# Value and output gate of a recurrent mixer's second half computed as one pair, with Strassen's scheme on two of eight chunks

## The chip, the cores and the metric

The kernel runs on one core of one Trainium2 chip. Its time is device time in microseconds (us) from the launch to the end of the program; "before" is the median of three runs. Besides there is one profiled execution, whose trace gives the start and the duration of each instruction of the engines: TensorE for matmuls (PE, its weight loads PEld), VectorE (DVE), ScalarE (ACT), GpSimd (POOL) and SyncE (SP), which here issues the transfers.

## What is computed

One layer of a decoder trunk on 256 tokens of 2048 features, all in float32. Cut to what matters:

```
h = rmsnorm(x, norm_mix_g)
u = h @ w_in                                  # 2048 x 12288
c_g, b_g, xa, za, q, fl, iv, og, ga, gb = split(u)
ya = b_g * causal_dwconv3(c_g * xa, conv_w) * silu(za)
o  = hgrn2_chunked(silu(q), kk, iv, log_f)    # kk and log_f from fl
yb = rmsnorm(o per head) * hg_norm_g * silu(og)
m  = sigmoid(ga) * (ya @ w_a_out) + sigmoid(gb) * (yb @ w_b_out)
x  = x + m @ w_o
x  = x + sigmoid(rmsnorm(x) @ w_ple_gate) * (p @ w_ple_proj)
return rmsnorm(x, final_norm_g)
```

The value `iv` and the output gate `og` of the recurrence are each 1024 wide. The kernel computes the eight fields of width 1024 in two halves of 512 columns.

## The kernel before, in words

**Groups, chunks, positions.** Each product with a weight matrix is cut into groups of 512 output columns, and a group into chunks of 256 rows of the weights (two k-tiles of 128). The list `groups` (lines 172 to 184) holds them in order: four projections PP, then f, q, iv, og, c, xa, za, b of the first half (j = 0), the same of the second half (j = 1), the merge gates ga and gb with the products A and B behind them, four groups O, and the late gates PG and GP. Each chunk is a position of `steps`; the main loop (line 1217) runs over the positions.

**Two halves of a number.** A float32 matrix is multiplied in three passes. `split` (lines 133 to 160) makes of a chunk of weights (128 x 1024) a rounded part `whi` on ACT (line 154) and the remainder `wlo` on DVE (line 155). The tokens exist as such a pair too. A plain chunk is 2 k-tiles x 2 token tiles x 3 matmuls (whi with xh, wlo with xh, whi with xl) of 128 x 128 by 512 columns, 12 in all (line 1156).

**Buffers and lead.** Raw weights come through three buffers of 1 MB (`load`, line 103), two chunks each. The pairs whi/wlo have four buffers in pool wp, so that a split waits until the matmuls of four positions before are over. `ahead` (line 1147) says how many positions the splits run ahead of the matmuls: LEAD = 3. In the range `gates` (line 212: from twelve positions before the first pair of merge gates to eight behind the last) a fifth pair of buffers is used, in the pool tmp2: at positions divisible by 5 (`more`, MORE = 1), and the lead is 4 there.

**Pairs by Strassen's scheme.** The merge gates ga and gb of j = 1, 2, 3 are computed together (kind GG, program GATES, line 42): two groups, eight chunks of rows. An entry such as `(0, 2)` is two plain chunks (2 and 3) of gate 0; an entry `("S", c)` is chunk c of both gates as a 2 x 2 block matrix (two k-tiles by two gates) times the 2 x 2 blocks of tokens, with seven products instead of eight, in four parts with 6, 3, 6 and 6 matmuls (`pair_products`, line 1166; its matmuls have line 1178). For it, `combine_weights` (line 162) makes differences and sums of the weight blocks on DVE (lines 166, 169, 170), in place and in a tile t2, and part 1 splits t2, half as wide. `forms_of_x` (line 750) loads the tokens of the chunks that are so treated, scales them on ACT (line 763) and makes four combinations and their pairs hi/lo on DVE and ACT (`forms`, lines 729 to 748). The products go to four accumulators "g" and four "s" in PSUM; `sums` (line 773) adds them up on DVE (line 769) as they become complete, after one copy on ACT (line 782), and hands each gate on.

**Epilogues.** When a group's last chunk is through, its epilogue starts as a generator; `advance` (line 1139) lets each one do a step per position (in an "S" entry at every second part), queued behind the newest split. `ep_iv` (line 405) scales the value into a tile v, `ep_og` (line 411) makes silu of the gate and goes over into `hgrn` (line 419), the recurrence of four heads: exponentials, element-wise products into tiles X (two of tag X, two of the ybT tiles, line 432), small matmuls on PE (lines 457, 590, 612 to 614), masks, norm, a turn through HBM, and the result ybT. It uses the tiles a, both, aoff (lines 437 to 441) and y (line 517) of pool tmp1. The second half's recurrence runs beside the groups c, xa, za, b.

The order of an engine's work is that of the program; the transfers are issued by SP in theirs (`ask_ahead`, line 1158).

Of the kernel before, what the change touches and what calls it, by code (L numbers as in the profile page):

```python
# [9 lines left out]
F32 = mybir.dt.float32  # L10
F32R = mybir.dt.float32r
# [4 lines left out]
P = 128  # L16
# [7 lines left out]
CW = 512  # L24
# [15 lines left out]


GATES = ("S", 0), (0, 2), ("S", 1), (1, 2), ("S", 4), (0, 6), ("S", 5), (1, 6)
LATE = (0, 4), ("S", 0), (0, 6), ("S", 1), (2, 3), ("S", 2), (1, 4), (1, 6)


# [6 lines left out]
def hybrid_kernel(ctx, tc, xT, x, pT, prm, gfin, masks, w_in, w_a, w_b, w_o, w_pg, w_pp, out):  # L52
# [28 lines left out]
    def nm(s):  # L81
        uid[0] += 1
        return f"{s}_{uid[0]}"
# [49 lines left out]
    def split(pos, c0=0, c1=2 * CW):  # L133
        part = part_of[pos]
        src = load(pos)[:, part % 2, :]
        if joint[pos]:

            src = load(pos)[:, part == 3, :]
            if part == 1:
                src, c1 = half[unit_of[pos]], CW  # L140

        pool, n = (pools["late"], 6) if (pos - state.get("late", len(steps))) % 10 < 6 and "late" in state else (wp, 4)
        if more(pos) and pos % (4 + MORE) < MORE:
            pool, n = pools[more(pos)], MORE
        if pos not in parts:
            parts[pos] = tuple(
                pool.tile([P, 2 * CW], F32R, tag=tag, bufs=n, name=nm(tag)) for tag in ("whi", "wlo")
            )
        hi, lo = parts[pos]
        s = slice(c0, c1)  # L150
        with ExitStack() as order:
            for i in state["before"].pop() if state.get("before") else ():
                order.enter_context(tc.issue_after(i))
            a = nc.scalar.activation(out=hi[:, s], in_=src[:, s], func=AF.Copy)  # L154
            v = nc.vector.tensor_tensor(  # L155
                out=lo[:, s], in0=src[:, s], in1=hi[:, s].bitcast(F32), op=ALU.subtract
            )
        state["splits"] = (a.ins, v.ins)
        if joint[pos] and part == 0:
            combine_weights(pos)  # L160

    def combine_weights(pos):

        b = load(pos).rearrange("p i (k c) -> p (i k) c", k=2)
        t2 = half[unit_of[pos]] = pools["tmp2" if pos in gates else "tmp3"].tile([P, CW], F32, tag="t2", bufs=2 if pos in gates else 1, name=nm("t2"))
        nc.vector.tensor_tensor(  # L166
            out=b[:, 0:4:3, :], in0=b[:, 0:3:2, :], in1=b[:, 3:4, :].to_broadcast([P, 2, CW]), op=ALU.subtract
        )
        nc.vector.tensor_tensor(out=t2, in0=b[:, 2, :], in1=b[:, 0, :], op=ALU.add)  # L169
        nc.vector.tensor_tensor(out=b[:, 1, :], in0=b[:, 1, :], in1=t2, op=ALU.subtract)  # L170
# [1 line left out]
    groups = []  # L172
    groups += [("PP", j, w_pp, j, "pT") for j in range(4)]
    for n, (kind, j) in enumerate(IN_ORDER):
        if j == 0 or kind not in ("ga", "gb"):
            groups.append((kind, j, w_in, n, "hT"))
        elif kind == "ga":
            groups.append(("GG", j, w_in, n, "hT", GATES))
        if kind == "gb":
            groups.append(("A", j, w_a, j, "yaT"))  # L180
            groups.append(("B", j, w_b, j, "ybT"))
# [24 lines left out]
    last_group = len(steps) - w_pg.shape[2]  # L206


    LEAD, MORE = 3, 1
    of_kind = lambda *kinds: [pos for pos, (gi, c) in enumerate(steps) if groups[gi][0] in kinds]  # L210
    gates, late = of_kind("GG"), of_kind("PG")[0]
    gates = range(gates[0] - 12, gates[-1] + 9)

    def more(pos):

        return "tmp2" if pos in gates else None

    TOKENS, NORM = 10, 13
    FIRST = 6

    praw = t4()[:, : 2 * T]
# [180 lines left out]
        plain_times(psum, sg, qt)  # L402
        state["qT", j] = yield from turned(qt, 5, t4("qT", 1))

    def ep_iv(j, psum):
        v = t4("v", 1)
        scaled(psum, v)
        state["v", j] = v
        yield
# [316 lines left out]
        yield  # L726


    def forms(op, pool, tag, r, chunks):


        n = len(chunks)
        f = t4()[:, : 4 * n * P]
        a11, a12, a21, a22 = (r[:, :, k, t * P : (t + 1) * P] for t in range(2) for k in range(2))
        s1, s2, s3, s4 = (f[:, i * n * P : (i + 1) * n * P].rearrange("p (u t) -> p u t", u=n) for i in range(4))
        nc.vector.scalar_tensor_tensor(out=s1, in0=a21, scalar=-1.0, in1=a22, op0=ALU.mult, op1=ALU.subtract)
        nc.vector.scalar_tensor_tensor(out=s2, in0=s1, scalar=-1.0, in1=a11, op0=ALU.mult, op1=ALU.subtract)
        yield
        nc.vector.tensor_tensor(out=s3, in0=a11, in1=a21, op=ALU.subtract)
        nc.vector.tensor_tensor(out=s4, in0=a12, in1=s2, op=ALU.subtract)  # L740
        yield
        hi, lo = (pool.tile([P, 4 * n * P], F32R, tag=tag + x, bufs=1, name=nm(tag + x)) for x in "hl")
        nc.scalar.activation(out=hi, in_=f, func=AF.Copy)
        nc.vector.tensor_tensor(out=lo, in0=f, in1=hi.bitcast(F32), op=ALU.subtract)
        for u in range(n):
            for i in range(4):
                s = slice((n * i + u) * P, (n * i + u + 1) * P)
                state["S", op, chunks[u], i] = hi[:, s], lo[:, s]

    def forms_of_x():  # L750

        joined = sorted(c for u, c in GATES if u == "S")
        for n in range(0, len(joined), 2):
            chunks = joined[n : n + 2]
            raw = t4()
            r = raw.rearrange("p (u k t) -> p u k t", u=2, k=2)
            for u in range(2):
                nc.sync.dma_start(out=r[:, u], in_=xT[:, 2 * chunks[u] : 2 * chunks[u] + 2, :])
            for u in range(2):
                yield  # L760
                for k in range(2):
                    h = r[:, u, k, :]
                    nc.scalar.activation(out=h, in_=h, func=AF.Identity, scale=gain(PRM_GMIX, 2 * chunks[u] + k))
            yield
            yield from forms("hT", pools["tmp2"], f"Sx{n}", r, chunks)
            yield

    def add(out, x, y):
# [32 lines left out]
    def ep_pair(j, e, left):  # L801

        def tiles_of():
            state["ga", j], state["gb", j] = t4("ga", 1), t4("gb", 1)
            return state["ga", j], state["gb", j]

        def then(q, g):
            for t in range(NT):
                s = slice(t * CW, (t + 1) * CW)
                nc.scalar.activation(  # L810
                    out=g[:, s], in_=g[:, s], func=AF.Sigmoid, scale=state["rstd1"][:, t : t + 1]
                )

        yield from sums(e, left, tiles_of, then)

    def ep_a(j, psum):
        g = state["ga", j]
# [26 lines left out]
    def ep_o(j, psum):  # L844
# [18 lines left out]
        if j < 2:  # L863
            for c in range(4):
                h = x1[:, c * T : (c + 1) * T]
                nc.scalar.activation(out=h, in_=h, func=AF.Identity, scale=gain(PRM_GPLE, j * 4 + c))
            hi, lo = (x[:, j * 4 : j * 4 + 4, :].rearrange("p k t -> p (k t)") for x in state["x1T"])
            nc.scalar.activation(out=hi, in_=x1, func=AF.Copy)
            nc.vector.tensor_tensor(out=lo, in0=x1, in1=hi.bitcast(F32), op=ALU.subtract)
            yield  # L870
            chunks = [c for u, c in LATE if u == "S" and c // 2 == j]
            r = x1.rearrange("p (u k t) -> p u k t", u=2, k=2)[:, : len(chunks)]
            yield from forms("x1T", pools["tmp3"], f"So{j}", r, chunks)
            return
        for c in range(4):
            put(state["x1T"], j * 4 + c, x1[:, c * T : (c + 1) * T], gain(PRM_GPLE, j * 4 + c))
# [269 lines left out]

    def ahead(pos):

        return LEAD + min(max(pos - late - 4, 0) // 3, 5) + MORE * (more(pos + LEAD) is not None and more(pos + LEAD + MORE) == more(pos + LEAD))

    def product(psum, op, k, t, hi, lo, first, last, which=(0, 1, 2)):

# [64 lines left out]
    for pos, (gi, c) in enumerate(steps[:last_group]):  # L1217
# [25 lines left out]
            load_x(pos + 2)  # L1243
        if pos == 4:
            begin()
        if 0 <= pos - NORM < 4:
            add_squares(pos - NORM)
        if pos == NORM + 3:
# [5 lines left out]
        if program:  # L1254
            program = program[0]
            if c == (0, 0):
                total = products_of(program)
                left, banks = dict(total), {}
            if c == (min(n for n, (u, _) in enumerate(program) if u == "S"), 0):
                active.append({"GG": ep_pair, "GP": ep_gates_late}[kind](j, banks, left))  # L1260
            pair_products(c, program, opname)
            ask_ahead()
            if not joint[pos] or c[1] % 2:
                advance()
            if kind == "GP" and c in ((1, 1), (3, 1)):
                load_projection(1 + c[0] // 2)
            continue
# [32 lines left out]
        if c == nch - 1:  # L1300
# [3 lines left out]
            if kind == "ga" and j == 0:  # L1304
                finish()
                second_part()
                active.append(forms_of_x())
                step(active[-1])
            if kind == "O" and j == 0:
                state["x1T"] = operand(big, "x", KT)  # L1310
# [103 lines left out]
```

## Time and profile before

| | |
|---|---|
| runs before (median, lowest, highest) | 814.6, 814.54, 814.64 us |
| the profiled execution, its own time | 814.02 us |
| its span, first to last instruction | 812.2 us |
| granted TensorE clock, mean | 0.996 |
| PE, PEld, DVE, ACT, POOL busy | 802.9, 667.5, 625.9, 463.5, 91.1 us |
| HBM read, written | 173.97 MB, 13.63 MB |

Spans are counted from the first instruction. A row of the timeline gives the start, the time taken, engine, line and operation, then what is written and what is read, with shapes; in brackets stands how long the engine was idle before and what released it. A row with x3 or the like is several instructions merged. In the views by group the last numbers are busy time, mean duration and idle time ahead of the group. Matmuls overlap in the trace, so that a duration of 0.39 us is no measure of their pace; the distance of their starts is.

### The profile page before, as it was taken

Reading aid. Unit: us, or ns where it says so; the run is one execution under the profiler, and the core shown is the slowest. Engines: PE = TensorE matmul, PEld = TensorE weight load, DVE = VectorE, ACT = ScalarE, POOL = GpSimd, SP = SyncE. Lnnn points to the kernel's source line nnn. Section 1 sums busy time; section 2 is a strip of 40 time slices with the busy share of each in tenths; the row PEclk is TensorE's granted clock in tenths of the full one; section 3 lists DMA queues with packets and bytes.
Section 4 is the critical chain, followed back from the end, with each engine's and each line's share of the span. In section 5 each row is a group of like instructions: output and inputs, shape, how many; then the busy total and the mean of one; then the engine's idle time right before and its main releaser. Section 6 shows DMA issues by size and latency. Waiting matters only on the chain.

```text
span 812.2 us, 10984 instructions
## 1 busy us (share of the span) xinstructions
PE 802.9 (99%) x4199; PEld 667.5 (82%) x4199; DVE 625.9 (77%) x737; ACT 463.5 (57%) x607; POOL 91.1 (11%) x74
## 2 busy tenths in 40 slices
PE   9999999999999999999999999999999999999995
PEld 7888888888888888888888888888888888888885
DVE  5747697967766488967767998998997657679895
ACT  7667465555555465565664554564564456665652
POOL 1000045400000055200001000100100000002012
PEclk9999999999999999999999999999999999999998
DMA  9979656747767555647764774774866687887542
GB/s 339 372 276 342 224 170 208 230 167 238 257 234 255 184 185 201 214 155 261 271 239 146 225 268 148 250 258 157 259 230 230 215 304 245 295 301 270 201 144 105
DMA packets 46565, 188.33 MB, mean 232 GB/s; under 512 B 5296, under 2 KB 14768, under 8 KB 31408
## 3 DMA queue, kind: packets, MB, share of 16 engines
q1 hardware_dynamic: 46368, 187.36, 67.5%
q8 instruction: 33, 0.54, 0.3%
q10 hardware_dynamic: 144, 0.26, 0.1%
q14 instruction: 20, 0.16, 0.1%
HBM read 173.97 MB, written 13.63 MB: 231 GB/s over the span
## 4 chain that ended last, share of the span: by engine, by line
PE 88%; DVE 5%; DMA 3%; ACT 1%; issue 1%; SPq 0%; POOL 0%; ACTq 0%; POOLq 0%; DVEq 0%
PE g L1156 70%; PE g L1178 11%; PE s L1178 4%; DMA raw<-in_w_pg 2%; DVE wlo L155 2%; PE s L1156 1%; PE s L457 1%; ACT whi L154 1%; DVE raw L166 1%; DMA raw<-in_w_pp 0%; DVE t L920 0%; DVE xs L921 0%; DMA turn<-t 0%; DVE t L169 0%; DVE t L938 0%
## 5 line engine op out<-in xcount | busy, mean ns | idle before, releaser
L155 DVE TENSOR_TENSOR wlo<-raw,whi 128x1024 fp32r<-128x1024 f32 (+1 forms) x310 | 384.4, 1255 | 156.3 <-ACT whi L154 154.9
L154 ACT ACTIVATE whi<-raw 128x1024 fp32r<-128x1024 f32 (+1 forms) x310 | 320.0, 1049 | 250.7 <-PE g L1156 197.4
L1156 PE MATMUL g<-wlo,xh 128*128 128x512 f32 (+1 forms) x656 | 251.9, 384 | 0.0
L1156 PE MATMUL g<-whi,xl 128*128 128x512 f32 (+1 forms) x656 | 251.7, 384 | 0.0
L1156 PE MATMUL g<-whi,xh 128*128 128x512 f32 (+1 forms) x656 | 251.6, 385 | 0.0
L1156 PEld LDWEIGHTS g<-whi,xh 128*128 128x128 f32 x656 | 123.3, 188 | 24.5
L1156 PEld LDWEIGHTS g<-whi,xl 128*128 128x128 f32 x656 | 123.3, 188 | 24.5
L1156 PEld LDWEIGHTS g<-wlo,xh 128*128 128x128 f32 x656 | 123.3, 188 | 24.0
L1178 PE MATMUL g<-wlo,xh 128*128 128x512 f32 x166 | 64.6, 389 | 0.0
L1178 PE MATMUL g<-whi,xl 128*128 128x512 f32 x166 | 64.6, 389 | 0.0
L1178 PE MATMUL g<-whi,xh 128*128 128x512 f32 x166 | 64.4, 389 | 0.0
L1156 PE MATMUL g<-whi,mh 128*128 128x512 f32 x128 | 49.8, 389 | 0.0
L1156 PE MATMUL g<-wlo,mh 128*128 128x512 f32 x128 | 49.8, 389 | 0.0
L1156 PE MATMUL g<-whi,ml 128*128 128x512 f32 x128 | 49.6, 389 | 0.0
L154 ACT ACTIVATE whi<-t 128x512 fp32r<-128x512 f32 x15 | 9.5, 632 | 54.4 <-DVE t L169 54.4
L1178 PEld LDWEIGHTS g<-whi,xl 128*128 128x128 f32 x166 | 31.2, 188 | 6.5
L1178 PEld LDWEIGHTS g<-whi,xh 128*128 128x128 f32 x166 | 31.2, 188 | 6.5
L1178 PEld LDWEIGHTS g<-wlo,xh 128*128 128x128 f32 x166 | 31.1, 188 | 6.4
L832 POOL TENSOR_TENSOR t<-ga,gb 128x512 f32<-128x512 f32 x6 | 10.6, 1786 | 192.9 <-issue 118.1
L1156 PEld LDWEIGHTS g<-whi,ml 128*128 128x128 f32 x128 | 24.0, 188 | 5.0
L1156 PEld LDWEIGHTS g<-wlo,mh 128*128 128x128 f32 x128 | 24.0, 188 | 5.0
L1156 PE MATMUL g<-whi,yaTh 128*128 128x512 f32 (+1 forms) x74 | 28.0, 385 | 0.1
(250 smaller groups left out, 919.8 us busy)
## 6 DMA issues: line engine op xcount, KB each, us to landing
raw<-in_w_in SPq DMA_DIRECT2D x73, 1024.0 KB, 5.0
raw<-in_w_in SPq DMA_DIRECT2D x34, 512.0 KB, 6.6
raw<-in_w_o SPq DMA_DIRECT2D x16, 1024.0 KB, 6.0
raw<-in_w_pg SPq DMA_DIRECT2D x12, 1024.0 KB, 6.4
turn<-t SPq DMA_DIRECT2D x72, 128.0 KB, 2.7
t<-turn SPq DMA_DIRECT2D x18, 512.0 KB, 5.4
raw<-in_w_a SPq DMA_DIRECT2D x8, 1024.0 KB, 5.2
raw<-in_w_b SPq DMA_DIRECT2D x8, 1024.0 KB, 5.3
```

Of the source, the lines that this page charges most:

```text
L154: a = nc.scalar.activation(out=hi[:, s], in_=src[:, s], func=AF.Copy)
L155: v = nc.vector.tensor_tensor(out=lo[:, s], in0=src[:, s], in1=hi[:, s].bitcast(F32), op=ALU.subtract)
L166: nc.vector.tensor_tensor(out=b[:, 0:4:3, :], in0=b[:, 0:3:2, :], in1=b[:, 3:4, :].to_broadcast([P, 2, CW]), op=ALU.subtract)
L457: nc.tensor.matmul(heads(bk)[r, h, c if at is None else slice(at, at + 32)], key(h)[:, r], query(h)[:, c], start=True, stop=True, tile_pos ...
L832: (nc.vector if j == 3 else nc.gpsimd).tensor_tensor(out=spread(m, t), in0=blocks(ga[:, s]), in1=blocks(gb[:, s]), op=ALU.add)
L1156: nc.tensor.matmul(psum, a, b, start=first and n == 0, stop=last and n == 2)
L1178: nc.tensor.matmul(banks[name], x, y[:, s], start=k == total[name] and i == 0, stop=k == 1 and i == 2)
```

## The change

The groups iv and og of the second half (j = 1) become one pair of kind VG with the program INNER: chunks 0 and 1 by Strassen's scheme, the other six of each plain, 20 positions in place of 16. `forms_of_x` takes the program and its target as arguments; for VG it runs from the sixth position before the pair and writes into the half of yaT that is still unused. The tiles t2 lie in the recurrence's tiles both and aoff. A new epilogue `ep_inner` lets `sums` add up, and hands the value to `ep_iv` (scaled in place) and the gate to `ep_og`, both now from SBUF.

In a range `inner`, from six positions before the pair to its end, three more pairs whi/wlo are used at three of seven positions: the two X tiles, a with y, and the two ybT tiles of the second half. `ahead` lets the lead grow there from 3 to 6 by steps (position + LEAD must have reached the range's start, two and four positions behind it). `MORE` becomes a table: one pair for `gates`, as before, three for `inner`. Positions behind the pair move by four.

Its core:

```diff
+INNER = (0, 2), (0, 4), ("S", 0), (0, 6), ("S", 1), (1, 2), (1, 4), (1, 6)
...
-        if more(pos) and pos % (4 + MORE) < MORE:
-            pool, n = pools[more(pos)], MORE
+        places = [(pool, n, tag) for tag in ("whi", "wlo")]
+        n = len(MORE[more(pos)])
+        if pos % (4 + n) < n:
+            places = [(pools[name], 1 + (tag == "X"), tag) for name, tag in MORE[more(pos)][pos % (4 + n)]]
...
+        if more(pos) == "inner":
+            pool, tag, n = "tmp1", ("both", "aoff")[unit_of[pos] // 2 % 2], 1
...
-        if j == 0 or kind not in ("ga", "gb"):
+        if (kind, j) == ("iv", 1):
+            groups.append(("VG", j, w_in, n, "hT", INNER))
+        elif (kind, j) == ("og", 1):
+            continue
+        elif j == 0 or kind not in ("ga", "gb"):
...
-    LEAD, MORE = 3, 1
+    LEAD = 3
+    MORE = {
+        None: (), "gates": ((("tmp2", "whi"), ("tmp2", "wlo")),),
+        "inner": (
+            (("tmp1", "X"), ("tmp1", "X")), (("tmp1", "a"), ("tmp1", "y")), (("branch", "ybTh1"), ("branch", "ybTl1")),
+        ),
+    }
...
+    inner = of_kind("VG")
+    inner = range(inner[0] - 6, inner[-1] + 1)
...
-        return "tmp2" if pos in gates else None
-
-    TOKENS, NORM = 10, 13
+        return "gates" if pos in gates else "inner" if pos in inner else None
+
+    TOKENS, NORM, FORMS = 10, 13, inner[0]
...
-    def ep_iv(j, psum):
-        v = t4("v", 1)
+    def ep_iv(j, psum, v=None):
+        v = t4("v", 1) if v is None else v
...
+    def ep_inner(j, e, left):
+
+        def then(q, g):
+            halves = [g[:, A], g[:, B]]
+            after = ep_og(j, halves) if q else ep_iv(j, halves, g)
+            next(after)
+            active.append(after)
+
+        yield from sums(e, left, lambda: (t4("v", 1), t4()), then)
...
-        return LEAD + min(max(pos - late - 4, 0) // 3, 5) + MORE * (more(pos + LEAD) is not None and more(pos + LEAD + MORE) == more(pos + LEAD))
+        at, n = more(pos + LEAD), 0
+        while n < len(MORE[at]) and more(pos + LEAD + n + 1) == at and (at == "gates" or pos + LEAD >= inner[0] + 2 * n):
+            n += 1
+        return LEAD + min(max(pos - late - 4, 0) // 3, 5) + n
...
+        if pos == FORMS:
+            held = [x[:, 4:, :].rearrange("p k t -> p (k t)") for x in state["yaT"]]
+            active.append(forms_of_x(INNER, lambda n: lambda: held))
+            step(active[-1])
...
-                active.append({"GG": ep_pair, "GP": ep_gates_late}[kind](j, banks, left))
+                active.append({"GG": ep_pair, "GP": ep_gates_late, "VG": ep_inner}[kind](j, banks, left))
```

More of the change, by code (lines that the diff above doesn't have):

```diff
@@ L142, in split @@
         pool, n = (pools["late"], 6) if (pos - state.get("late", len(steps))) % 10 < 6 and "late" in state else (wp, 4)
-        if more(pos) and pos % (4 + MORE) < MORE:
-            pool, n = pools[more(pos)], MORE
+        places = [(pool, n, tag) for tag in ("whi", "wlo")]
+        n = len(MORE[more(pos)])
+        if pos % (4 + n) < n:
+            places = [(pools[name], 1 + (tag == "X"), tag) for name, tag in MORE[more(pos)][pos % (4 + n)]]
         if pos not in parts:
             parts[pos] = tuple(
-                pool.tile([P, 2 * CW], F32R, tag=tag, bufs=n, name=nm(tag)) for tag in ("whi", "wlo")
+                pool.tile([P, 2 * CW], F32R, tag=tag, bufs=n, name=nm("w" + x)) for (pool, n, tag), x in zip(places, ("hi", "lo"))
             )
@@ L164, in combine_weights @@
         b = load(pos).rearrange("p i (k c) -> p (i k) c", k=2)
-        t2 = half[unit_of[pos]] = pools["tmp2" if pos in gates else "tmp3"].tile([P, CW], F32, tag="t2", bufs=2 if pos in gates else 1, name=nm("t2"))
+        pool, tag, n = ("tmp2", "t2", 2) if pos in gates else ("tmp3", "t2", 1)
+        if more(pos) == "inner":
+            pool, tag, n = "tmp1", ("both", "aoff")[unit_of[pos] // 2 % 2], 1
+        t2 = half[unit_of[pos]] = pools[pool].tile([P, CW], F32, tag=tag, bufs=n, name=nm("t2"))
         nc.vector.tensor_tensor(
@@ L726, in ep_gb, with forms @@
         yield
-    def forms(op, pool, tag, r, chunks):
+    def forms(op, made, r, chunks):
         n = len(chunks)
@@ L741, in forms @@
         yield
-        hi, lo = (pool.tile([P, 4 * n * P], F32R, tag=tag + x, bufs=1, name=nm(tag + x)) for x in "hl")
+        hi, lo = made()
         nc.scalar.activation(out=hi, in_=f, func=AF.Copy)
@@ L748, in forms, with form_tiles, forms_of_x @@
                 state["S", op, chunks[u], i] = hi[:, s], lo[:, s]
-    def forms_of_x():
-        joined = sorted(c for u, c in GATES if u == "S")
+    def form_tiles(pool, tag, n=2):
+        return lambda: tuple(pool.tile([P, 4 * n * P], F32R, tag=tag + x, bufs=1, name=nm(tag + x)) for x in "hl")
+    def forms_of_x(program, made):
+        joined = sorted(c for u, c in program if u == "S")
         for n in range(0, len(joined), 2):
@@ L764, in forms_of_x @@
             yield
-            yield from forms("hT", pools["tmp2"], f"Sx{n}", r, chunks)
+            yield from forms("hT", made(n), r, chunks)
             yield
@@ L872, in ep_o @@
             r = x1.rearrange("p (u k t) -> p u k t", u=2, k=2)[:, : len(chunks)]
-            yield from forms("x1T", pools["tmp3"], f"So{j}", r, chunks)
+            yield from forms("x1T", form_tiles(pools["tmp3"], f"So{j}", len(chunks)), r, chunks)
             return
@@ L1306, in hybrid_kernel @@
                 second_part()
-                active.append(forms_of_x())
+                active.append(forms_of_x(GATES, lambda n: form_tiles(pools["tmp2"], f"Sx{n}")))
                 step(active[-1])
```

## The prediction

> **What bounds the kernel now.** The page comes first. Under the span stand each engine's busy time, its share of the span and its instructions.
>
> ```profile
> span 812.2 us, 10984 instructions
> ...
> PE 802.9 (99%) x4199; PEld 667.5 (82%) x4199; DVE 625.9 (77%) x737; ACT 463.5 (57%) x607; POOL 91.1 (11%) x74
> ```
>
> A busy PE proves little by itself, so the second view is that of the waits of PE (engine, line, what it waited for, us in total, times, longest), the third the chain that ended last (start, us, what).
>
> ```profile
> PE s L1034 <- PEq L1403: 0.8, 1, 0.8
> ```
>
> ```profile
> 178.21 138.73 PE g L1156 x612
> ...
> 359.11 84.33 PE g L1156 x372
> 443.44 0.68 PE s L1178 x3
> ...
> 478.80 5.44 PE g L1178 x24
> 484.24 21.76 PE g L1156 x96
> ...
> 609.36 108.59 PE g L1156 x479
> ```
>
> PE waits once in the whole execution, 0.8 us for its warm-up at the start. From 178 to 718 the chain is PE behind PE: no transfer and no split of weights is late. (The rest of the chain passes over other engines, but the waits view has no further wait of PE.) So the pace of the matmuls sets the end, and the pace is in the chain: 21.76 / 96 = 0.2267 us for one of 512 columns, and 84.33 / 372 gives the same. Nothing but fewer matmuls can shorten this kernel there, and any wait of PE is added in full.
>
> The Trainium skill, "Perfetto Trace Analysis", section Identifying the Most-Contended Engine, says that the busy share of matmuls is no good measure and that weight-load busy time is a better one; by it the 82% of PEld leaves headroom, and fewer matmuls might return nothing. The trace agrees that 99% proves little, but the waits view and the constant 0.2267 us speak against headroom here.
>
> **The gain.** A plain chunk of 256 rows for two gates takes 2 k-tiles x 2 token tiles x 2 gates x 3 (hi/lo) = 24 matmuls; by Strassen's scheme it is seven products, 21. The trace already holds the same thing: the pair of gates from 443.44 to 484.24 has four such chunks of eight and takes 40.80 us, where two plain groups take 2 x 21.76 = 43.52: 2.72 us for four, 0.68 each. Two chunks: 6 x 0.2267 = **1.36 us**.
>
> The Trainium skill, "TensorE: Matmul & The Clock Gate", section Back-to-back issue gap, gives some 131 ns for a sustained matmul of 512 columns; by it six would be an estimated 0.79 us and the time 813.8. The row of this kernel decides: 0.2267.
>
> **What it costs.** All of it is on DVE, ACT and SP, so it costs nothing unless a split comes late. The windows (us, then busy time and count of PE, PEld, DVE, ACT and POOL, granted TensorE clock, DMA share, GB/s) are: today's value and output gate; the recurrence of the second half with the four groups beside it; the existing pair.
>
> ```profile
> 240.63:284.15 43.52, 43.52 (x194) 36.04 (x192) 25.61 (x23) 22.87 (x26) 1.96 (x1) 1.00 0.66 218
> 284.15:378.00 93.85, 93.85 (x697) 78.16 (x696) 76.07 (x95) 55.44 (x84) 29.03 (x20) 1.00 0.59 196
> 443.28:484.08 40.80, 40.80 (x181) 33.78 (x180) 38.53 (x39) 24.36 (x27) 3.53 (x2) 1.00 0.73 244
> ```
>
> The added instructions have rows in the existing pairs: subtraction, T2 and third combination (L166, L169, L170), the half-size split, the sums (L769), the copy out of PSUM (L782), the forms of x (L736 to L744, L763) and their load (L758). First the groups of the existing pair's window (count, busy us, mean ns, idle before and its releaser), then one line's own view (ns min/median/max), rows of the timeline (start, us), and the groups of the window of value and output gate.
>
> ```profile
> L166 DVE TENSOR_TENSOR raw<-raw 128x1024 f32<-128x1024 f32 x3 | 3.7, 1225 | 0.1
> ...
> L155 DVE TENSOR_TENSOR wlo<-t,whi 128x512 fp32r<-128x512 f32 x3 | 2.1, 692 | 0.2
> L169 DVE TENSOR_TENSOR t<-raw 128x512 f32<-128x512 f32 x3 | 2.1, 692 | 0.1
> L170 DVE TENSOR_TENSOR raw<-raw,t 128x512 f32<-128x512 f32 x3 | 2.1, 692 | 0.1
> L154 ACT ACTIVATE whi<-t 128x512 fp32r<-128x512 f32 x3 | 1.9, 632 | 12.5 <-DVE t L169 12.5
> ```
>
> ```profile
> L769 DVE TENSOR_TENSOR gb<-gb,s x9: 681/683/1218, 479.5 to 609.8; 128x512 f32<-128x512 f32 x6, 128x1024 f32<-128x1024 f32 x3
> ```
>
> ```profile
> 406.73 1.70 ACT L763 ACTIVATE t<-t,prm_t 128x256 f32<-128x256 f32 x4
> ```
>
> ```profile
> 408.46 0.43 DVE L736 SCALAR_TENSOR_TENSOR t<-t 128x256 f32<-128x256 f32 x1 [0.18 <-ACT t L763]
> ...
> 413.08 1.22 DVE L744 TENSOR_TENSOR Sx0l<-t,Sx0h 128x1024 fp32r<-128x1024 f32 x1
> ```
>
> ```profile
> L155 DVE TENSOR_TENSOR wlo<-raw,whi 128x1024 fp32r<-128x1024 f32 x17 | 20.8, 1224 | 17.7 <-ACT whi L154 17.5
> L154 ACT ACTIVATE whi<-raw 128x1024 fp32r<-128x1024 f32 x16 | 16.9, 1059 | 19.6 <-PE g L1156 19.6
> ```
>
> DVE: combining 2 x (1.225 + 2 x 0.692) = 5.2; each chunk's splits are three and a half instead of four, 2 x (0.692 - 1.224) = -1.1; sums 6 x 0.683 + 1.22 = 5.3; forms 4 x 0.43 + 1.22 = 2.9, of which the load's place (sixth position before the pair) puts nearly all ahead of the window. Together 12.3: 25.6 + 12.3 = 37.9 us if all fell into the new window of 42.16, 90%. The existing pair runs at 38.53 of 40.80, 94%, with one extra pair of tiles, and PE doesn't wait there. ACT gains 1.70 + 1.06 (L743, by the whi of its shape) + 0.63 (L782, by a half-size whi) - 2 x (1.059 - 0.632) = 2.5 on 22.9. Price: nothing while this cover holds; with it gone, each us that a split is late is a us of PE.
>
> How much cover, before the added lead? The last fence, of the window of value and output gate, says it: ACT idled 19.6 us, all of it until PE gave a buffer back, and DVE 17.7 us behind ACT. The splits are as early as four pairs of tiles allow. Three more pairs raise the lead from three positions to six (it grows at positions 75, 77 and 79, while the pair begins at 84), 3 x 12 x 0.2267 = 8.2 us more. DVE's burst in a Strassen chunk is 3 x 1.224 + 0.692 + 2.6 = 7.0 us for 21 x 0.2267 = 4.8 us of PE; two chunks fall behind by 4.4 us, with a plain unit (5.4 us of PE, 2.4 of DVE) between them to catch up.
>
> The added wait: ACT's half-size whi waits for T2 (12.5 us over three in the row above, some 4 each); behind it in ACT's queue stand the next two splits and the epilogues, and DVE waits for those. Two of them are 8 us of ACT's free 19.6, spread over a lead of as much. Taken as nothing; bounds 0 and 8, the range keeps a part.
>
> **SP and the forms' load.** Bytes of weights are the same; each Strassen chunk is three issues instead of one, and two transfers of x are new.
>
> ```profile
> 397.31 0.90 SPq L758 DMA_DIRECT2D t<-in_xT  x2
> ```
>
> ```profile
> DMA to landing us min/median/max: 5.3/5.6/5.8
> ```
>
> Two issues take 0.9 us on SP and land after 5.3 to 5.8. The gain of x stands on ACT one position (2.72 us) behind the issue, so ACT may wait about 3 us, with the splits of the pair's first chunks behind it. PE then holds splits of five positions, 13.6 us. Nothing, then; the forms are needed some eleven positions later.
>
> **What the tiles cost elsewhere.** The first half's recurrence ends with the puts of ybT, the second's begins with y:
>
> ```profile
> 208.02 1.67 DVE L266 SCALAR_TENSOR_TENSOR ybTl<-t,prm_t,ybTh 128x256 fp32r<-128x256 f32 x4
> ```
>
> ```profile
> 287.39 1.22 DVE L518 TENSOR_TENSOR y<-b,tot 128x1024 f32<-128x1024 f32 x1
> ```
>
> Between these X, a, y, both and aoff are dead, as are the second half of yaT and the second ybT pair. The new pair's last use of them is over before 284; its first (positions 78 and 79, split some three to four positions ahead) comes after 208. The recurrence begins one position later against its neighbours, since the last two sums (2 x 0.68) stand ahead of its gate. What is late next there?
>
> ```profile
> 332.00 1.21 DVE L155 TENSOR_TENSOR wlo<-raw,whi 128x1024 fp32r<-128x1024 f32 x1
> ```
>
> ```profile
> 337.35 0.39 PE L1156 MATMUL g<-whi,xh 128*128 128x512 f32 x1
> ```
>
> ```profile
> 313.23 0.41 DVE L493 TENSOR_TENSOR X<-t,qT 128x256 f32<-128x256 f32 x1
> ```
>
> ```profile
> 316.95 1.29 PE s L457 x96
> ```
>
> The tightest split of that stage ended at 333.2 and PE took it at 337.35: 4.1 us. The tightest input of its own small matmuls, X, was ready 3.3 us early. Its matmuls move with it, so that distance stays. 1.4 us more DVE work fits into both. Value: 0, bounds 0 and +1.
>
> The sum, against the profiled execution: 814.02 (span 812.2) - 1.36 = 812.66. That execution lay 0.58 under the median of 814.6 (runs 814.54 to 814.64), so for a median: 814.6 - 1.36 = **813.24**, 0.17% less.
>
> **The rivals.**
>
> *A burst too dense* (PE waits in the new pair, under 3 us in all). For it: 7.0 us of DVE for 4.8 of PE. Against: 4.4 us of arrears against 8.2 us of added lead and a stage that is 59% busy now. It would eat the gain, at the likeliest 1 to 1.4 us: 814.2 to 814.6.
>
> *No headroom used:* PE's pace isn't what ends last there, and six matmuls return nothing: 814.6. The 2.72 us of the existing pair speak against it.
>
> *The three later pairs lose their lead* (slower). They have almost no reserve:
>
> ```profile
> 453.52 4.63 DVE L155 TENSOR_TENSOR wlo<-raw,whi 128x1024 fp32r<-128x1024 f32 x4 [0.46 <-ACT whi L154]
> ```
>
> ```profile
> 455.52 0.39 PE L1178 MATMUL s<-whi,Sx0h 128*128 128x512 f32 x1
> ```
>
> The first of these four splits ends near 454.75 and PE uses it at 455.52: 0.77 us. The program grows by four positions, and which position gets the fifth pair of tiles is counted by position modulo 5, so their turn falls one position later against the chunks. If that cost them one plain position of lead, each would wait 2.72 - 0.77 = 1.95 us: 814.6 - 1.36 + 3 x 1.95 = **819.1**. It decides from 0.77 us on. Against: five pairs in rotation give the same lead in whatever phase once they all turn, and the stage is entered twelve positions after they begin.
>
> **How the numbers follow.** Forecast (no new wait) 0.82, own range 812.9 to 813.7; dense burst 0.08; no headroom 0.03; lost lead 0.07. For 8 in 10 the forecast's own range nearly does; with half of the burst it is 812.9 to 814.2. What a measurement can tell from no change is taken as 0.2%, 1.63 us, so the border of faster is 812.97, only 0.27 below the forecast, about half of what the profiled execution lay from the median. Faster gets 0.10 out of the forecast's 0.82; the other 0.72, the burst and no headroom make same 0.83; lost lead is slower, 0.07.
>
> **What would show it.** Right: PE's instructions 4199 - 6 = 4193, the new pair's 186 matmuls in 42.16 us, still one wait of PE in the waits view, DVE 12 us busier in all. Wrong: a wait of PE for wlo L155 or an X in 238 to 285, a chain that leaves PE before 700, or a wait in the three later pairs; or matmuls whose distance isn't 0.2267.

## The result, and the profile after

The changed kernel is slower: 817.88 us (817.45 to 818.38, six runs) against 814.57 (814.38 to 814.68, six runs) of the kernel before beside it, ratio 1.0041 with an interval of 1.0028 to 1.0054. The forecast was 813.24 with a range of 812.9 to 814.2: the wrong side, and out of the range by 3.7 us. (The profiled executions lie 4.36 us apart, 818.38 and 814.02. Of this 0.93 us is there before any changed work has run: the first small matmul of the recurrence starts at 136.90 us, before at 135.97. That is the spread of the start; e4 below, the same up to there, has 136.06.)

The page of the changed kernel, span and engines:

```profile
span 816.6 us, 11017 instructions
...
PE 805.5 (99%) x4193; PEld 666.2 (82%) x4193; DVE 637.2 (78%) x759; ACT 468.3 (57%) x617; POOL 91.9 (11%) x74
```

PE has six matmuls fewer, 4193, and DVE is 11.3 us busier in all: the work is what was counted. Yet PE is busy for 2.6 us more, with less to do, while the weight loads fell by 1.3: a part of each late start counts as busy, as is worked out below. PE's waits (engine, line, what it waited for, us in total, times, longest):

```profile
PE g L1214 <- DVE wlo L158: 1.0, 2, 0.7
PE s L1067 <- PEq L1443: 0.8, 1, 0.8
PE g L1192 <- issue: 0.4, 1, 0.4
PE s L1214 <- DVE wlo L158: 0.2, 1, 0.2
PE g L1192 <- ACT mh L871: 0.2, 1, 0.2
PE g L1214 <- ACT whi L157: 0.2, 1, 0.2
```

One row has become six, of which one, that of the warm-up, was there before. (Lines have moved: the split is 157 and 158, a pair's matmuls 1214, plain ones 1192.) Where the waits are, the chain that ended last tells. It is PE behind PE up to the new pair, leaves PE inside it and comes back to PE there (start, us, what):

```profile
241.72 8.17 PE g L1214 x36
...
250.88 1.56 ACT whi L157 x2
...
263.97 0.70 DVE t L175
264.77 0.63 ACT whi L157
...
271.27 16.16 PE g L1214 x70
```

From 250 to 271 the chain runs over ACT and DVE, the splits, and back to PE. The window of the pair (us, then busy time and count of PE, PEld, DVE, ACT, POOL, granted clock, DMA share, GB/s), from its first matmul to the first behind it:

```profile
241.56:287.27 45.71, 44.18 (x188) 34.30 (x186) 36.38 (x42) 23.07 (x28) 5.28 (x4) 1.00 0.54 185
```

45.71 us for 186 matmuls, not 42.16: **3.55 us lost here**, at full clock. The waits view shows only 1.4 us of that for line 1214. A matmul's record is 0.39 us long while the next may start after 0.2267, so up to 0.16 us of each late start is covered by the record of the matmul before. The Trainium skill, "Perfetto Trace Analysis", section Summary: the profiler window per engine type, says that the end of a TensorE record is an estimate; the trace agrees, and the distance of starts is the measure.

Two smaller losses lie elsewhere. Four late starts between 650.91 and 653.11, in the first output group, make 0.83 us, and one in the group za 0.57, each beyond the pace. Six matmuls fewer, and 3.55 + 0.83 + 0.57 more, would be 3.59 us; the medians differ by 3.31.

**The main loss.** ACT in the changed kernel around the pair's first Strassen chunk:

```profile
240.95 1.06 ACT L762 ACTIVATE yaTh<-t 128x1024 fp32r<-128x1024 f32 x1 [0.78 <-DVE t L759]
247.19 1.06 ACT L157 ACTIVATE whi<-raw 128x1024 fp32r<-128x1024 f32 x1 [5.18 <-PE g L1214]
249.91 2.01 ACT L157 ACTIVATE whi<-raw 128x1024 fp32r<-128x1024 f32 x2 [1.66 <-PE g L1214]
251.83 0.61 ACT L157 ACTIVATE whi<-t 128x512 fp32r<-128x512 f32 x1
```

and DVE:

```profile
243.63 0.68 DVE L175 TENSOR_TENSOR t<-raw 128x512 f32<-128x512 f32 x1
...
252.48 0.69 DVE L158 TENSOR_TENSOR wlo<-t,whi 128x512 fp32r<-128x512 f32 x1 [5.90 <-ACT whi L157]
```

T2 was ready at 244.31. The half-size split that needs it ran at 251.83, 7.5 us later, and ACT was idle for 4.5 of them (2.88 up to 247.19, then 1.66), waiting for PE to give buffers back, for splits that are needed later. The order of the splits in ScalarE's queue of the built program says why (position, line, written and read):

```
88 L157 whi_2206<-raw_2151 128x1024
92 L157 whi_2305<-raw_2173 128x1024
93 L157 whi_2326<-raw_2173 128x1024
91 L157 whi_2289<-raw_2151 128x1024
89 L157 whi_2236<-t_357_2210 128x512
90 L157 whi_2264<-raw_2151 128x1024
```

The pair begins at position 84; 88 to 91 are the four parts of its first Strassen chunk, and 89 is the one whose split is half as wide. Ahead of it stand the splits of 92, 93 and 91, so the queue isn't in the order of the positions. They are the three whole splits of the trace above, at 247.19 and (two merged) at 249.91. 92 uses a with y, which position 85 used last, and 93 the ybT tiles of 86; PE finished those at 247.0 and 249.7, which is where ACT goes on. Up to there the lead had grown as forecast: at position 87 wlo was ready 11.1 us before PE reached the position. At 89 it was ready 0.6 us before, at 90 too late: the wlo of 90 ended at 255.80, and its matmul started at 255.85, 0.45 us behind the one before.

**The first output group.** It is preceded by the last turn of the tokens m through HBM. SP before (start, time taken, engine, line, operation):

```profile
609.90 16.12 SPq L121 DMA_DIRECT2D raw<-in_w_o  x4
633.08 1.77 SPq L301 DMA_DIRECT2D turn<-t  x4
634.95 0.40 SPq L121 DMA_DIRECT2D raw<-in_w_o  x1
637.47 0.34 SPq L303 DMA_DIRECT2D t<-turn  x1
638.95 0.33 SPq L121 DMA_DIRECT2D raw<-in_w_o  x1
```

and after:

```profile
613.81 21.23 SPq L122 DMA_DIRECT2D raw<-in_w_o  x5
637.11 1.80 SPq L320 DMA_DIRECT2D turn<-t  x4
642.81 0.35 SPq L122 DMA_DIRECT2D raw<-in_w_o  x1
643.33 0.34 SPq L322 DMA_DIRECT2D t<-turn  x1
```

Five transfers of w_o now go out ahead of the turn's write, not four. The sixth then stands between the write and the read and waits for its buffer until 642.81, so that the read goes 6.2 us behind the write's start, where it had been 4.4. DVE takes up what was read, before and after:

```profile
642.15 1.25 DVE L307 STREAM_TRANSPOSE t<-t 128x1024 f32<-128x1024 f32 x1 [0.51 <-DMA t<-turn]
```

```profile
649.13 1.25 DVE L326 STREAM_TRANSPOSE t<-t 128x1024 f32<-128x1024 f32 x1 [3.62 <-DMA t<-turn]
```

From the start of the write that is 9.1 us before and 12.0 after: the tokens m come 2.9 us later, 1.8 of it by the late issue of the read, the rest in its transfer. The rival of the lost lead had named the cause, the count of positions modulo 5, at another place.

**The group za.** PE's weight loads there:

```profile
354.08 0.19 PEld L1192 LDWEIGHTS g<-wlo,xh 128*128 128x128 f32 x1 [0.84 <-issue]
```

"Issue" means that the profile shows nothing that the engine waited for.

### The profile page after: what moved, and what is told of

It reads as the page before. It is cut to its first block, busy times and chain, and to the rows that moved or that the text cites. A ratio compares the mean times of both kernels' runs of the same rounds, so it can differ in the third digit from the quotient of the medians.

```text
span 816.6 us, 11017 instructions
## 1 busy us (share of the span) xinstructions
PE 805.5 (99%) x4193; PEld 666.2 (82%) x4193; DVE 637.2 (78%) x759; ACT 468.3 (57%) x617; POOL 91.9 (11%) x74
## 4 chain that ended last, share of the span: by engine, by line
PE 86%; DVE 7%; issue 2%; DMA 2%; ACT 2%; POOL 0%; ACTq 0%; POOLq 0%; SPq 0%; DVEq 0%
PE g L1192 66%; PE g L1214 14%; PE s L1214 4%; DVE wlo L158 3%; ACT whi L157 1%; DMA raw<-in_w_pg 1%; DMA t<-turn 1%; PE s L1192 1%; PE s L476 1%; DVE t L953 1%; DVE raw L172 1%; DMA raw<-in_w_pp 1%; DVE t L792 0%; DVE xs L954 0%; DVE t L971 0%
## 5 line engine op out<-in xcount | busy, mean ns | idle before, releaser
L1192 PE MATMUL g<-wlo,xh 128*128 128x512 f32 (+1 forms) x592 | 227.0, 384 | 0.4 <-issue 0.4
L1192 PE MATMUL g<-whi,xl 128*128 128x512 f32 (+1 forms) x592 | 226.8, 383 | 0.0
L1192 PE MATMUL g<-whi,xh 128*128 128x512 f32 (+1 forms) x592 | 226.8, 384 | 0.0
L1192 PEld LDWEIGHTS g<-wlo,xh 128*128 128x128 f32 x592 | 111.3, 188 | 22.4 <-issue 0.8
L1192 PEld LDWEIGHTS g<-whi,xl 128*128 128x128 f32 x592 | 111.2, 188 | 22.0
L1192 PEld LDWEIGHTS g<-whi,xh 128*128 128x128 f32 x592 | 111.2, 188 | 21.9
L1214 PE MATMUL g<-wlo,xh 128*128 128x512 f32 x218 | 85.1, 390 | 1.0 <-DVE wlo L158 1.0
L1214 PE MATMUL g<-whi,xl 128*128 128x512 f32 x218 | 84.9, 389 | 0.0
L1214 PE MATMUL g<-whi,xh 128*128 128x512 f32 x218 | 84.7, 389 | 0.0
L1214 PEld LDWEIGHTS g<-wlo,xh 128*128 128x128 f32 x218 | 40.9, 188 | 10.3 <-DVE wlo L158 1.8
L1214 PEld LDWEIGHTS g<-whi,xl 128*128 128x128 f32 x218 | 40.9, 188 | 8.5
L1214 PEld LDWEIGHTS g<-whi,xh 128*128 128x128 f32 x218 | 40.9, 188 | 8.4
L1192 PEld LDWEIGHTS g<-whi,mh 128*128 128x128 f32 x128 | 24.0, 188 | 5.7 <-ACT mh L871 0.6
```

The source lines that it names most:

```text
L1192: nc.tensor.matmul(psum, a, b, start=first and n == 0, stop=last and n == 2)
L1214: nc.tensor.matmul(banks[name], x, y[:, s], start=k == total[name] and i == 0, stop=k == 1 and i == 2)
```

## The experiments

Four theories were put to the chip. *Order* (O): the loss in the pair comes from the later splits ahead of the half-size one in ACT's queue. *Density* (D), its rival: the pair's DVE and ACT work is too dense whatever its order. *Phase*: the output group's loss comes from the fifth pair of tiles changing place. *Instruction supply* (I): the gap in za is PE's queue running out of instructions behind the recurrence's burst of small matmuls. The runs of the kernel before beside the first four experiments have a median of 814.44 us, beside the last three 814.32.

**e1_order.** Inside the range `inner`, each split is queued behind those before it:

```diff
+            for i in state["splits"] if more(pos) == "inner" else ():
+                order.enter_context(tc.issue_after(i))
```

> The change with one thing added: inside the range of the new pair each split is queued behind the split of the position before, on ScalarE and on VectorE. Theory O (order): in the changed kernel ScalarE's queue holds the splits of positions 92, 93 and 91 ahead of the half-size split of position 89 and waits there for TensorE; that alone dries the pair out. Then the matmul distances in the pair are all 0.227 us, the 3.3 us of gaps there vanish and the time is about 814.5 us. Theory D (dense): VectorE's burst in a Strassen chunk is too long in whatever order; then 2 us of gaps or more remain in the pair and the time stays at 816.5 or above. By both the 0.8 us of gaps in the first output group remain.

Measured 814.65 us, ratio 1.0002 (0.9993 to 1.0011). ACT (lines are two further here), then the pair's window:

```profile
244.30 0.64 ACT L159 ACTIVATE whi<-t 128x512 fp32r<-128x512 f32 x1 [2.40 <-DVE t L177]
```

```profile
241.70:283.86 42.16, 42.16 (x188) 34.91 (x186) 35.62 (x42) 22.84 (x28) 4.12 (x4) 1.00 0.58 198
```

The half-size split now runs the moment T2 is ready, 244.30, and the pair takes 42.16 us, the forecast's figure to the digit, though the same work stands in it (42 instructions of DVE, 28 of ACT, as after). So with the tiles as they are, order alone is the cause of the loss in the pair. (The edit orders the splits on DVE too; the rows above show that it was ACT that DVE waited for.) The gaps in za and in the output group are still there, and they eat the six matmuls.

**e2_phase.** In the range `gates` the place is counted four positions back, as in the kernel before:

```diff
+        at = pos - 4 * (more(pos) == "gates")
-        if pos % (4 + n) < n:
+        if at % (4 + n) < n:
```

> The change with the fifth pair of tiles of the merge gates counted from four positions earlier, so that its turns fall on the same chunks as before the change. Theory P (phase): the shifted turn let one raw chunk of w_o be freed a split earlier, so that on SyncE a later raw transfer, which waits for a later split, stands ahead of the second half of the last turn of m; its operand comes some 3 us late and TensorE has gaps of 0.8 us in the first output group. Then this kernel has no gap there and takes about 817.1 us; the gaps of the pair stay at 3.3 us. If the late transfer was chance, nothing changes: 817.9.

Measured 817.19 us, ratio 1.0033 (1.002 to 1.0045). SP:

```profile
613.44 16.12 SPq L122 DMA_DIRECT2D raw<-in_w_o  x4
636.63 1.77 SPq L321 DMA_DIRECT2D turn<-t  x4
638.50 0.40 SPq L122 DMA_DIRECT2D raw<-in_w_o  x1
641.03 0.34 SPq L323 DMA_DIRECT2D t<-turn  x1
```

Four transfers, the turn, one transfer, the read, as before the change; the output group has no gap left, while the pair's are unchanged. The phase is the cause of the 0.83 us.

**e3_both.** Both edits together.

> Both of the former edits. Theories O and P together: no gap in the pair and none in the first output group; 817.9 - 3.3 - 0.8 = 813.8 us, or 813.2, six matmuls under the kernel before, if the rest of the difference (0.7 us of a gap without releaser in the group za, 0.8 us at the start) is chance. Theory D: 816 or above.

Measured 813.75 us, ratio 0.9991 (0.9983 to 1.0). The two add up: against e1 the phase brought 0.90 us, against e2 the order 3.44. Behind the start one gap is left, in za:

```profile
349.51 0.40 PE L1195 MATMUL g<-whi,xh 128*128 128x512 f32 x1
350.43 0.50 PE L1195 MATMUL g<-wlo,xh 128*128 128x512 f32 x1 [0.52 <-issue]
```

0.92 us from start to start, 0.69 over the pace. The two rows also show the reading trap again: the view puts 0.52 in brackets.

**e4_no_extra.** The pair without the three extra pairs of tiles and the added lead:

```diff
-        "inner": (
-            (("tmp1", "X"), ("tmp1", "X")), (("tmp1", "a"), ("tmp1", "y")), (("branch", "ybTh1"), ("branch", "ybTl1")),
-        ),
+        "inner": (),
```

> The pair by Strassen's scheme without the three more pairs of tiles: four pairs in rotation and a lead of three positions throughout. Theory O: without free tiles no later split can be started ahead of the half-size one, the order is kept, and the pair has gaps of 0 to 2 us (arrears of 4.4 us against a lead of 5.6 us): 814.5 to 816.5. Theory D: the lead was what held the gaps to 3.3 us; without it they are 5 us or more, and the time 819.5 or above.

Measured 818.01 us, ratio 1.0045 (1.0032 to 1.0057). The window of the pair, and its waits:

```profile
240.73:286.89 46.16, 43.35 (x188) 34.51 (x186) 41.17 (x45) 25.99 (x31) 3.64 (x3) 1.00 0.60 205
```

```profile
PE g L1212 <- DVE wlo L158: 1.5, 1, 1.5
PE s L1212 <- DVE wlo L158: 1.1, 1, 1.1
```

With the lead of three, ACT's queue keeps the order of the positions, and yet the pair loses 4.0 us. ACT, then DVE:

```profile
251.04 0.63 ACT L157 ACTIVATE whi<-t 128x512 fp32r<-128x512 f32 x1 [3.34 <-DVE t L175]
```

```profile
247.74 1.23 DVE L158 TENSOR_TENSOR wlo<-raw,whi 128x1024 fp32r<-128x1024 f32 x1 [1.18 <-ACT whi L157]
...
250.26 0.69 DVE L175 TENSOR_TENSOR t<-raw 128x512 f32<-128x512 f32 x1
...
252.32 2.28 DVE L404 TENSOR_TENSOR_SCAN b<-carry,t 128x1024 f32<-128x1024 f32 x1
```

Here T2 itself is late: DVE forms it at 250.26, ready only at 250.95, where e1's split could begin at 244.30. Ahead of it DVE had waited for a split of ACT, which worked from 239.1 to 247.7 without a pause (splits, forms and an epilogue with its exponentials); behind it stands the scan at 252.32 ahead of the next wlo, for which PE waits. So density is real once the cover is gone, on ACT and DVE together. Neither theory had this run's time: O had said 814.5 to 816.5 and no more than 2 us of loss, D 819.5 or above. The extra tiles are worth 818.01 - 814.65 = 3.4 us if the order holds; with the order that the change's program got, they are worth nothing (818.01 against 817.88).

**e5_both_fewer.** e3 with six of the warm-up matmuls at the start left out, whose result nothing uses; this moves PE's stream by twelve instructions (each matmul has a weight load) and so asks about supply:

```diff
-WARM = (64,) * 51 + (CW,) * 3 + (64,) * 8
+WARM = (64,) * 45 + (CW,) * 3 + (64,) * 8
```

> Both edits and six of the small warm-up matmuls at the start left out (they make nothing that is used). Theory I (instructions): the gap of 0.7 us in the group za, which follows the recurrence's densest burst of small matmuls and has no releaser, is TensorE waiting for instructions; the trace has TensorE's part of the instruction queue fetch 16 KB right behind that burst, and the burst stands 13 instructions later in the stream than before the change. Six matmuls and their weight loads fewer ahead of it put it back: no gap behind that burst, 813.75 - 0.7 = 813.0 us. If the gap is something else (a late operand), it stays and the time is 813.7.

Measured 812.85 us (812.39 to 814.68, eleven runs), ratio 0.9984 (0.9975 to 0.9993): 0.18% under the kernel before. Its waits and the pair:

```profile
PE s L1070 <- PEq L1446: 0.8, 1, 0.8
PE g L1195 <- ACT whi L160: 0.3, 1, 0.3
```

```profile
241.11:283.27 42.16, 42.16 (x188) 34.91 (x186) 35.04 (x40) 22.74 (x27) 3.69 (x4) 1.00 0.57 193
```

The second wait is that of the first weights, near 5 us. Behind it no matmul is late. The gap in za is gone. The median is 0.90 us under e3's; set against the kernel before beside each, e3 gained 0.69 and e5 1.47, 0.78 more.

**e6_before_more** and **e7_before_fewer.** The kernel before with six unused warm-up matmuls more (57), and six fewer (45).

> The kernel before with six more small warm-up matmuls. Theory I: the burst stands 12 instructions later in the stream, as in the changed kernel, and a gap of some 0.7 us appears behind it in the group za, at 346 to 350 us, though nothing else of the kernel is changed: 814.4 + 0.7 = 815.1 us, beside up to 0.3 us for the longer warm-up. If the gap comes from the changed order of the recurrence, there is none, and the time is 814.4 to 814.7.

> The kernel before with six small warm-up matmuls fewer, as a control of what the warm-up alone does: by theory I no gap behind the burst of the second half (it stands 12 instructions earlier; a gap elsewhere is possible, since every burst moves), and 814.1 to 814.5 us.

Measured 814.46 us, ratio 1.0003 (0.9994 to 1.0012), and 814.41, ratio 1.0000 (0.999 to 1.0009), neither with a gap. e7 is the control for e5: leaving out the warm-up matmuls is worth nothing that shows by itself, so e5's gain over e3 is put down to the gap, 0.69 us in e3's trace. e6 missed what theory I expected of it; the section on the hardware comes back to this.

## Why the prediction was wrong

**What bounds the kernel: right.** PE's pace sets the end, and any wait of PE is added in full: three places of waiting account for the difference to within 0.3 us. The prediction's own sign of being wrong came, a wait of PE for wlo between 238 and 285.

**The gain of 1.36 us: right.** e5 is 1.47 us under the kernel before, with no late start left. By the 131 ns per matmul of the Trainium skill ("TensorE: Matmul & The Clock Gate", section Back-to-back issue gap), it would have been an estimated 0.79. The interval of e5, 0.6 to 2.0 us, holds both; what decides is the pace in the pair, where 186 matmuls in 42.16 us are 0.2267 each.

**The work added: right.** DVE 11.3 us for 12.3 counted; the extra tiles gave a margin of 11.1 us; the recurrence's start moved without a late matmul before za. For the transfer of x the prediction allowed a wait of some 3 us on ACT. The scaling of x (L786) didn't wait, but a split ahead of it did, for a transfer of weights. In the changed kernel:

```profile
229.83 2.01 ACT L157 ACTIVATE whi<-raw 128x1024 fp32r<-128x1024 f32 x2 [3.28 <-DMA raw<-in_w_in]
...
234.67 1.70 ACT L786 ACTIVATE t<-t,prm_t 128x256 f32<-128x256 f32 x4
```

Around it, from 222 to 236, transfers of 1 MB of weights took a median of 7.5 us to land, against 4.9 over the whole run. PE had no late start there, so it cost nothing.

**The step that failed:** "The added wait: ACT's half-size whi waits for T2 [...] behind it in ACT's queue stand the next two splits and the epilogues [...] Taken as nothing". The prediction asked what stands behind the waiting instruction and not what stands ahead of it, and it took the queue to be in the program's order, which the description of the kernel above says too ("The order of an engine's work is that of the program"); for ScalarE of the changed kernel that isn't so. In the built kernel three later splits stood ahead, two of which had to wait for PE first, and what was taken as nothing cost PE 3.55 us. The 8.2 us of added lead were there and were spent on them: a lead counts only if the queue serves the earliest need first. With the order kept (e1) the step is worth nothing, as was said, and 4.4 us of arrears fit under the lead. Without the tiles (e4) they don't: that is the cover that the prediction said the step depended on, priced at 3.4 us.

**The rival "a burst too dense"** had the right place, the wlo of the new pair, the wrong mechanism, and a price too small: 1 to 1.4 us at the likeliest and under 3 us in all, against 3.55. Its bound came from sums of DVE time, and ACT's idling on a buffer isn't in such a sum.

**The rival "lost lead"** had the right cause, the phase modulo 5, and the wrong place. The merge gates kept their margin, and PE has no late start in the three pairs. DVE and PE after:

```profile
457.39 5.77 DVE L158 TENSOR_TENSOR wlo<-raw,whi 128x1024 fp32r<-128x1024 f32 x5 [0.46 <-ACT whi L157]
```

```profile
459.38 0.39 PE L1214 MATMUL s<-whi,Sx0h 128*128 128x512 f32 x1
```

The first of five ends near 458.62 and is used at 459.38: 0.76 us, as before. What was at stake was the far end of the range `gates`, where its last turns decide when a buffer of raw weights comes free and so what SP has ahead of a turn through HBM. The prediction had named SP's queue as one that each moved step passes, and looked only at the issues near the pair.

**The third loss,** 0.57 us in za, is in no step and no rival.

Why the order was lost isn't settled. It goes with the extra tiles: the program without them (e4) keeps it. That more free buffers let the later splits count as ready sooner when the queues were built is likely, and argued only.

## What to carry to other kernels

A deeper rotation of buffers brings lead only if each engine's queue stays in the order of need: read the built order of every in-order queue around the edit, ahead of a waiting instruction as well as behind it, and pin it where it matters. Where something is chosen by a counter modulo n, an edit that shifts the counter moves every later choice; follow it to the last one that hangs on it, transfers included. Measure a matmul engine's loss by the distance of starts, against a window of known count, since the waits view showed less than half of it here.

## What was not expected of the hardware

The gap in za. It comes in all five kernels with the pair and the full warm-up (after and e1 to e4) at the same matmul, the 2137th of PE's stream, 0.57 to 0.91 us over the pace, some 5.5 us from the start of a burst of small matmuls (the recurrence's, 128 x 32 and the like, 160 with a weight load each). In the records of the DMA queue q8, which carries instructions in pieces of 16 KB, the piece behind the burst is fetched 2.9 to 3.3 us after the burst's beginning in these kernels and in e5, but 1.3 to 1.8 us in before, e6 and e7, which have no gap. The fetch takes 0.9 to 1.4 us. q8's records alone don't make the case: in the five kernels the fetch has ended 1.3 to 1.6 us before the late matmul starts, and behind the same burst of the first half, near 163 us, it begins 4.6 to 5.1 us after the burst's beginning, in all nine kernels, without a gap.

The Trainium skill, "Runtime: NRT & Kernel Launch", section Instruction fetch mechanics, says that instructions come in blocks of 16 KiB that the sequencer fetches ahead, and that crossing a block's border is mostly hidden. The trace agrees on the size; a border behind a dense burst may not have been hidden here.

For supply speak the fixed place in the stream, the missing releaser, and e5: there the fetch is as late (3.2 us), PE's stream is twelve instructions shorter, and the gap is gone. Against it stand the ends of the fetches, and e6, where a shift the other way made none, though its fetch was early, so that it may have had nothing to show. So supply is supported and not proven, and why the fetch begins later in the kernels with the pair stays open.
